# Prompt attention: four places for a head's queries and keys, sent for three heads ahead

## The chip, the cores and the metric

One core of a Trainium2 chip runs the whole program. The metric is the device time of one execution in microseconds; three runs of the kernel before are at hand, and one further execution was profiled.

## The reference, cut to what matters

The program is one step of a small decoder: a convolution mixer, shared keys, values and forget gates, and one attention layer, for a prompt of 1024 positions and for 8 single new positions that attend to a paged cache. The change lies in the prompt's attention, 16 heads of 64 features, in float32:

```python
def fox_attend(q, k, v, cq, ck, q_pos, k_pos):
    ...
    s = jnp.einsum('bqhd,bkhd->bhqk', qi.astype(jnp.float32), kf) * scale
    s = s + jnp.swapaxes(ci, 1, 2)[..., :, None] - ckh[..., None, :]
    s = jnp.where((k_pos[None, :] <= pi[:, None])[None, None], s, -jnp.inf)
    p = jax.nn.softmax(s, axis=-1)
    return jnp.einsum('bhqk,bkhd->bqhd', p, vf)

def fox_mixer(x, k, v, cq, ck, q_pos, k_pos, norm_g, w_in, q_g, w_out):
    ...
    o = fox_attend(q, k, v, cq, ck, q_pos, k_pos).reshape(b, t, ATTN_DIM)
    return x + (o * jax.nn.silu(z)) @ w_out
```

Here `c` is the running sum of the forget gates' logarithms, and `z` the output gate.

## The kernel before

Ahead of the attention, the projections leave queries, keys, values, gates and the sums `c` in HBM (`qt_scr`, `kt_scr`, `vt_scr`, `z_scr`, `c_scr`), the float32 ones as a high and a low part. The prompt's attention then runs from about 973 to 1333 us, and the output projection follows.

Each head goes through two passes. `first(h)` has 8 steps, one for a block of 128 queries: score matmuls into PSUM (L1165, L1166, and a mask, L1168), a row maximum on VectorE (L1169), an exponential with its sum on ScalarE (L1171). After four blocks, `logsum` turns maximum and sum into a row of normalisers, and SyncE sends it to two partitions of the head's `q2` (L1193, source `lt`). `second(h)` has 6 steps on transposed scores: matmuls into `st` (L1228, L1229, masks L1234, L1236), the exponential into `pt` on ScalarE (L1238), its high part `ph` on GpSimd (`pool_copy`, L198), its low part `pl` on GpSimd or VectorE (L1242), and three steps later (`LAGW`) the matmuls with the values into `po` (`weigh`, L1208, L1209). `po` goes to `og` (L1212, L1213); at the end of each odd head `og` is multiplied by the gates `sz` (L1255) and split for the output projection (L1257, L1258).

The two passes are laid side by side by a pattern of 14 turns (`PAT`): 8 first steps and 6 second steps, with the first passes 13 steps ahead (`LEAD`). So `first(h+2)` begins three first steps after `second(h)` has begun.

A head's `q1, q2, k1, k2` (16 KB of each partition) are one place. Pool `h0` has two and pool `hd` one; head h takes `hd` when `h % 3 == 2`. `load_qk(h)` sends 8 transfers from SyncE's queue (L639): six of 256 KB, then 16 KB and 24 KB from `c_scr`. `load_rest(h)` sends the values `vh` (512 KB, two buffers, L644) and, for even h, the gates `sz` of two heads (512 KB, two buffers, L648). Both are written down together for head h+2 where `second(h)` begins.

The program is laid out by a compiler that orders each engine's instructions by what it reckons to be ready; the order written in the source is its priority. An engine runs its own list strictly in order. A tile waits for the last reader of the tile that had its memory before. The pools lie on one another in the order in which they are opened: `ld` (`sz`), `hd`, `wk` (`og`, `pt`, `ph`, `pl`, `tb`), and the output projection's pool (`wr`, `wb`, values of the cache) later takes the same memory.

Of the kernel before, what the change touches and what calls it, by code (L numbers as in the profile page):

```python
# [9 lines left out]
F32 = mybir.dt.float32  # L10
F32R = mybir.dt.float32r
# [8 lines left out]
P = 128  # L20
D = 1024
T = 1024
# [3 lines left out]
NH = 16  # L26
# [50 lines left out]
QORD = (0, 4, 1, 5, 2, 6, 3, 7)  # L77
PS_S = 2
PS_O = 1
PTB = 4  # L80
PHB = 5
VHB = 2
LAGW = 3
PLO = ((0, 0), (0, 2), (1, 0), (1, 6))
# [41 lines left out]
def f32(ap):  # L126
    return ap.bitcast(F32)
# [7 lines left out]
def tile_step(ctx, tc, xt, st, stT, vecs, cwT, win, wout, wqkv, wf, wbo, hvec, qgf, ck, cv, cf, pt,  # L135
# [16 lines left out]
    def table(name):  # L152
        tc.keep_in_program_order(S.preload_act_table_set(name))
# [475 lines left out]
    hd = h0 = None  # L629
    szs = {}  # L630

    def load_qk(h):
        pool = hd if h % 3 == 2 else h0
        q1, q2, k1, k2 = [pool.tile([P, 1024], F32R, tag=nm, name=nm) for nm in ("q1", "q2", "k1", "k2")]
        fs = slice(h * HD, (h + 1) * HD)

        for out, src in ((q1[0:HD], qt_scr[0, fs]), (k1[0:HD], kt_scr[0, fs]), (q1[HD:P], qt_scr[1, fs]), (k1[HD:P], kt_scr[0, fs]),
                         (q2[0:HD], qt_scr[0, fs]), (k2[0:HD], kt_scr[1, fs]), (q2[HD:HD + 4], c_scr[h, 0:4]), (k2[HD:HD + 6], c_scr[h, 4:10])):
            SY.dma_start(out=f32(out), in_=src)  # L639
        return q1, q2, k1, k2  # L640

    def load_rest(h):
        vh = hd.tile([P, 8, P], F32R, tag="vh", name="vh", bufs=VHB)
        SY.dma_start(out=f32(vh), in_=vt_scr[h].rearrange("(i p) f -> p i f", p=P))  # L644
        hp, e = divmod(h, 2)
        if e == 0:
            sz = szs[hp] = ld.tile([P, T], F32, tag="sz", name="sz")
            SY.dma_start(out=sz, in_=z_scr[hp])  # L648
        return vh

    qk0 = []

    def load0():
        nonlocal h0
        h0 = pat.enter_context(tc.tile_pool(name="h0", bufs=2, side="right", reuse_waits="tile"))
        qk0.extend([load_qk(0), load_qk(1)])
# [48 lines left out]
    with ExitStack() as pb:  # L705
# [374 lines left out]
        for n_, (kind, half) in enumerate(order):  # L1080
            ws, nxt = nxt, None
            if n_ + 1 < len(order):
                k2, h2 = order[n_ + 1]
# [38 lines left out]
    with pat:  # L1122
        ld = pat.enter_context(tc.tile_pool(name="ld", bufs=2, reuse_waits="tile"))
        hd = pat.enter_context(tc.tile_pool(name="hd", bufs=1, reuse_waits="tile"))
# [6 lines left out]
        def qbank(name):  # L1131
            if OBANK:
                return psO.tile([P, 512], F32, tag="o", name=name)
            return psQ.tile([P, 512], F32, tag="q", name=name)

        ogs = {}

        def load(h):
            return load_qk(h) + (load_rest(h),)


        off_ = []

# [1 line left out]
        def put_off(n, f):  # L1145
            off_.append([n, f])

        def catch_up(n=1):
            for x in list(off_):
                x[0] -= n  # L1150
                if x[0] < 0:
                    off_.remove(x)
                    x[1]()

        def first(h, q1, q2, k1, k2, vh):
            nm = sm.tile([P, 8], F32, tag="nm", name="nm")
            sr = sm.tile([P, 8], F32, tag="sr", name="sr")
            for qi in QORD:
                nk = (qi + 1) * P
                qsl = slice(qi * P, (qi + 1) * P)  # L1160
                ss = qbank("ss") if nk in SMF else psS.tile([P, 1024], F32, tag="s", name="ss")
                for b0 in range(0, nk, 512):
                    w = min(512, nk - b0)
                    lastb = b0 + w == nk
                    PE.matmul(ss[:, b0:b0 + w], q1[:, qsl], k1[:, b0:b0 + w], start=True, stop=False)  # L1165
                    PE.matmul(ss[:, b0:b0 + w], q2[0:HD + 4, qsl], k2[0:HD + 4, b0:b0 + w], start=False, stop=not lastb)  # L1166
                    if lastb:
                        PE.matmul(ss[:, qsl], identb, maskb, start=False, stop=True)  # L1168
                V.tensor_reduce(out=nm[:, qi:qi + 1], in_=ss[:, :nk], axis=AX.X, op=ALU.max, negate=True)  # L1169
                def expsum(ss=ss, nk=nk, qi=qi):  # L1170
                    S.activation(out=ss[:, :nk], in_=ss[:, :nk], func=AF.Exp, bias=nm[:, qi:qi + 1], accum_out=sr[:, qi:qi + 1])  # L1171

                put_off(DEXP, expsum)
                catch_up()
                if qi % 4 == 3:
                    put_off(DEXP + DLS, lambda qi=qi: logsum(h, qi // 4, nm, sr, q2))
                yield nk

        def logsum(h, c, nm, sr, q2):
            cs = slice(c * 4, c * 4 + 4)  # L1180
            S.activation(out=sr[:, cs], in_=sr[:, cs], func=AF.Ln)
            V.tensor_tensor(out=nm[:, cs], in0=nm[:, cs], in1=sr[:, cs], op=ALU.subtract)
            lc = sm.tile([P, 8], F32R, tag="lc", name="lc")
            V.tensor_copy(out=lc[:, 0:4], in_=nm[:, cs])
            V.tensor_tensor(out=lc[:, 4:8], in0=nm[:, cs], in1=f32(lc[:, 0:4]), op=ALU.subtract)

            def turn():
                ps = qbank("lt")
                PE.transpose(f32r(ps[0:8, 0:P]), lc, identr)
                lt = sm.tile([8, P], F32, tag="lt", name="lt")  # L1190
                S.copy(out=lt, in_=ps[0:8, 0:P])
                for a in range(2):
                    SY.dma_start(out=f32(q2[HD + 4 + a:HD + 5 + a, c * 512:(c + 1) * 512]).rearrange("a (t q) -> a t q", t=4), in_=lt[4 * a:4 * a + 4])  # L1193

            put_off(DLT, turn)

        def second(h, q1, q2, k1, k2, vh):
# [17 lines left out]
            for c in range(2):  # L1215
                po = psO.tile([P, 512], F32, tag="o", name="po")
                for j0 in range(0, 4 * c + 4, 2):
# [12 lines left out]
                    for o in range(0, off, 512):  # L1230
# [4 lines left out]
                        elif ds:  # L1235
                            PE.matmul(st[:, ds[0]:ds[0] + P], identb, maskt, start=False, stop=True)  # L1236
                    pt_, ph, pl = [wk.tile([P, 1024], dt, tag=nm, name=nm, bufs=b) for nm, dt, b in (("pt", F32, PTB), ("ph", F32R, PHB), ("pl", F32R, PHB))]
                    S.activation(out=pt_[:, :off], in_=st[:, :off], func=AF.Exp)  # L1238
# [14 lines left out]
            if e:  # L1253
                for a, b in ((0, 512), (512, 1024)):
                    (V if a // 512 in OGV else G).tensor_tensor(out=og[:, a:b], in0=og[:, a:b], in1=szs[hp][:, a:b], op=ALU.mult)  # L1255
                for a, b in ((0, 512), (512, T)):
                    S.copy(out=oa.hi(hp, a, b - a), in_=og[:, a:b])  # L1257
                    V.tensor_tensor(out=oa.lo(hp, a, b - a), in0=og[:, a:b], in1=f32(oa.hi(hp, a, b - a)), op=ALU.subtract)  # L1258

        hs = [qk0[h] + (load_rest(h),) for h in range(2)]  # L1260
        table("natural_log_exp_and_others")
        oa = Act("o")

        def firsts():
            for h in range(NH):
                yield from first(h, *hs[h])

        def seconds():
            for h in range(NH):
                if h + 2 < NH:  # L1270
                    hs.append(load(h + 2))
                yield from second(h, *hs[h])


        if MAN:
            pat.enter_context(tc.manual_schedule(engines={getattr(mybir.EngineType, e) for e in MAN.split()}))
        fs_, ss_, n = firsts(), seconds(), 0
        for _ in range(LEAD):
            next(fs_)
# [138 lines left out]
```

## Time and profile before

| what | us |
|---|---|
| median of 3 runs (lowest, highest) | 1462.08 (1460.68, 1472.82) |
| the profiled execution's own time | 1459.9 |
| span of its trace | 1458.2 |

The span is what the trace covers, from the first to the last instruction; 1.7 us of the execution lie around it. In the views, PE is TensorE's matmuls, PEld its weight loads, DVE VectorE, ACT ScalarE, POOL GpSimd, and SPq SyncE's queue, from which all transfers of this stage are sent. PEclk is the granted clock of TensorE as a share of 2.4 GHz. A window's row gives its bounds and length, the busy time of PE, PEld, DVE, ACT and POOL with the number of instructions, the granted clock, the DMA engines' busy share and GB/s. A matmul's end is modelled and matmuls are pipelined, so a busy PE isn't a PE at its peak.

### The profile page before, as it was taken

What the parts mean: (1) busy time and instruction counts of PE and PEld (TensorE: products, weight loads), DVE (VectorE), ACT (ScalarE), POOL (GpSimd) and SP (SyncE); (2) the same over time, 40 slices, a digit from 0 to 9 for tenths busy, and PEclk for the clock granted to TensorE, in tenths of its full rate; (3) what the DMA queues carried; (4) which work ended last, traced back from release to release, by engine and by line L of the source; (5) the groups of instructions that cost most, each with busy time, mean ns of one, the idle gap of its engine ahead of it and who ended that gap; (6) DMA issues with size and microseconds to landing.
All of it is one profiled execution on the core that took longest, in us unless ns stands there. A gap on an engine that the chain in (4) does not pass through costs nothing.

```text
span 1458.2 us, 21461 instructions
## 1 busy us (share of the span) xinstructions
PE 1292.8 (89%) x6543; PEld 1077.8 (74%) x6543; DVE 1132.5 (78%) x1844; ACT 734.1 (50%) x1922; POOL 803.9 (55%) x603
## 2 busy tenths in 40 slices
PE   5999999789999999998898899897988888887978
PEld 5999999777777777666776778786766666665766
DVE  6999999998735699989898999854656575667841
ACT  7676537646645666655642232135656565662100
POOL 4699987862210253456565565724545455567930
PEclk9999999999999999999998989997868798888979
DMA  5111001121334576878778888693444456423841
GB/s 206 56 59 59 30 29 34 30 75 41 130 125 145 158 225 203 229 250 272 231 251 273 277 272 268 211 241 91 111 96 101 92 133 133 101 48 118 286 139 37
DMA packets 155530, 213.95 MB, mean 147 GB/s; under 512 B 14057, under 2 KB 82281, under 8 KB 155399
## 3 DMA queue, kind: packets, MB, share of 16 engines
q1 hardware_dynamic: 137879, 202.09, 47.4%
q10 hardware_dynamic: 16896, 8.39, 2.0%
q0 software_dynamic: 640, 2.10, 0.5%
q8 instruction: 52, 0.85, 0.3%
q14 instruction: 63, 0.52, 0.1%
HBM read 165.22 MB, written 48.13 MB: 146 GB/s over the span
## 4 chain that ended last, share of the span: by engine, by line
PE 18%; DMA 10%; DVE 10%; issue 5%; SPq 4%; ACT 2%; POOL 1%; DVEq 0%; ACTq 0%; POOLq 0%
DMA k<-c_scr 4%; DVE vt L683 4%; DMA vt<-in_cv 3%; SPq L639 2%; PE st L1228 2%; PE st L1229 2%; PE ss L1166 2%; PE ss L1165 2%; DMA k<-kt_scr 2%; PE po L1208 1%; PE po L1209 1%; PE py L1312 1%; PE py L1314 1%; PE py L1313 1%; PE pz L1055 1%
## 5 line engine op out<-in xcount | busy, mean ns | idle before, releaser
L347 POOL TENSOR_TENSOR cvt<-cvt 128x512 f32<-128x512 f32 (+4 forms) x179 | 243.7, 1394 | 38.4 <-ACT cvt L343 35.5
L906 POOL TENSOR_TENSOR kh<-kh,qb 128x512 f32<-128x512 f32 x96 | 139.8, 1472 | 135.6 <-DMA kh<-in_ck 85.4
L352 DVE SCALAR_TENSOR_TENSOR acc<-u,cw,acc 128x512 f32<-128x512 f32 (+4 forms) x285 | 196.0, 742 | 0.1
L198 POOL TENSOR_SCALAR ph<-pt 128x896 fp32r<-128x896 f32 (+1 forms) x96 | 87.6, 921 | 175.9 <-ACT pt L1238 172.3
L1169 DVE TENSOR_REDUCE nm<-ss 128x1 f32<-128x768 f32 (+7 forms) x128 | 93.6, 751 | 110.4 <-PE ss L1168 97.5
L685 POOL TENSOR_TENSOR av<-av,vt 128x512 f32<-128x512 f32 x80 | 134.2, 1698 | 69.8 <-DVE vt L683 53.0
L1105 PE MATMUL pq<-wp,acth 128*128 128x512 f32 x384 | 160.1, 417 | 0.0
L1107 PE MATMUL pq<-wp,actl 128*128 128x512 f32 x384 | 156.4, 407 | 0.0
L1106 PE MATMUL pq<-wp,acth 128*128 128x512 f32 x384 | 156.2, 407 | 0.0
L683 DVE TENSOR_TENSOR vt<-vt,lg 128x512 f32<-128x512 f32 x112 | 133.8, 1228 | 7.8 <-DMA vt<-in_cv 7.6
L343 ACT ACTIVATE cvt<-u,cw 128x512 f32<-128x512 f32 (+4 forms) x195 | 126.1, 719 | 17.9 <-POOL cvt L347 9.4
L1171 ACT ACTIVATE ss<-ss,nm 128x768 f32<-128x768 f32 (+7 forms) x128 | 91.2, 713 | 44.5 <-DVE nm L1169 43.4
L1238 ACT ACTIVATE pt<-st 128x896 f32<-128x896 f32 (+1 forms) x96 | 75.4, 809 | 71.7 <-PE st L1229 46.6
L1242 POOL TENSOR_TENSOR pl<-pt,ph 128x384 fp32r<-128x384 f32 (+2 forms) x56 | 105.7, 1894 | 2.7
L1165 PE MATMUL ss<-k,q 128*128 128x512 f32 (+2 forms) x192 | 80.2, 425 | 23.7 <-DMA k<-kt_scr 14.6
L1166 PE MATMUL ss<-k,q 68*128 68x512 f32 (+2 forms) x192 | 74.3, 400 | 20.4 <-DMA k<-c_scr 17.7
L1107 PEld LDWEIGHTS pq<-wp,actl 128*128 128x128 f32 x384 | 75.2, 196 | 19.2 <-issue 0.8
L1105 PEld LDWEIGHTS pq<-wp,acth 128*128 128x128 f32 x384 | 75.8, 197 | 18.0 <-ACT hsq L826 0.8
L1106 PEld LDWEIGHTS pq<-wp,acth 128*128 128x128 f32 x384 | 75.7, 197 | 16.9 <-issue 0.2
L907 DVE TENSOR_REDUCE lg<-kh 128x8 f32<-128x512 f32 x128 | 82.7, 673 | 5.0 <-POOL kh L906 5.0
L1208 PE MATMUL po<-ph,vh 128*128 128x512 f32 x192 | 78.3, 411 | 5.8 <-DVE og L1213 4.0
L1228 PE MATMUL st<-q,k 128*128 128x512 f32 (+1 forms) x192 | 79.5, 422 | 3.0 <-ACT ss L1171 2.9
(337 smaller groups left out, 3788.7 us busy)
## 6 DMA issues: line engine op xcount, KB each, us to landing
kh<-in_ck SPq DMA_DIRECT2D x128, 256.0 KB
vt<-in_cv SPq DMA_DIRECT2D x128, 256.0 KB
wraw<-in_wqkv SPq DMA_DIRECT2D x56, 256.0 KB
wr<-in_win SPq DMA_DIRECT2D x24, 512.0 KB
q<-qt_scr SPq DMA_DIRECT2D x48, 256.0 KB
k<-kt_scr SPq DMA_DIRECT2D x48, 256.0 KB
vt_scr<-vx SPq DMA_DIRECT2D x32, 256.0 KB
vh<-vt_scr SPq DMA_DIRECT2D x16, 512.0 KB
```

The lines of the kernel that those rows point to most:

```text
L343: S.activation(out=t[:, :m], in_=u[:, lo + j:hi + j], func=AF.Copy, scale=cw[:, c, j:j + 1])
L347: G.tensor_tensor(out=pacc[:, :m], in0=pacc[:, :m], in1=t[:, :m], op=ALU.add)
L352: V.scalar_tensor_tensor(out=acc, in0=u[:, lo + jd:hi + jd], scalar=cw[:, c, jd:jd + 1], in1=acc, op0=ALU.mult, op1=ALU.add)
L683: V.tensor_tensor(out=heads(vt[x] if g else ax), in0=heads(vt[x]), in1=over_d(lg[:, p0:p0 + 8], P, 8), op=ALU.mult)
L685: (V if g % VDVE == 3 else G).tensor_tensor(out=ax, in0=ax, in1=vt[x], op=ALU.add)
L906: (V if g % 4 == 3 else G).tensor_tensor(out=kt, in0=kt, in1=qb, op=ALU.mult)
L1105: PE.matmul(ps, na.hi(k, t * P, P), ws[k][:, 0:512], start=(k == 0), stop=False)
L1106: PE.matmul(ps, na.hi(k, t * P, P), ws[k][:, 512:1024], start=False, stop=False)
L1107: PE.matmul(ps, na.lo(k, t * P, P), ws[k][:, 0:512], start=False, stop=(k == KT - 1))
L1165: PE.matmul(ss[:, b0:b0 + w], q1[:, qsl], k1[:, b0:b0 + w], start=True, stop=False)
L1228: PE.matmul(st[:, o:o + w], k1[:, js], q1[:, qs], start=(o % 512 == 0), stop=False)
L1242: (G if plo else V).tensor_tensor(out=pl[:, :off], in0=pt_[:, :off], in1=f32(ph[:, :off]), op=ALU.subtract)
```

## The change

The places become four: two in `h0`, two in `hd`. `load_qk` is written down for head h+3 where `second(h)` begins, after the first three heads have been sent for ahead of the loop. `load_rest` is split off, and is written down for head h+1 there, ahead of `load_qk`. To make room for 16 KB, `pt` has three buffers instead of four (4 KB less), `ph` and `pl` four instead of five (8 KB less), and `sz` one instead of two (4 KB less). No instruction is added or removed.

```diff
-PTB = 4
-PHB = 5
+PTB = 3
+PHB = 4
...
     def load_qk(h):
-        pool = hd if h % 3 == 2 else h0
-        q1, q2, k1, k2 = [pool.tile([P, 1024], F32R, tag=nm, name=nm) for nm in ("q1", "q2", "k1", "k2")]
+        pool = hd if h % 4 > 1 else h0
+        q1, q2, k1, k2 = [pool.tile([P, 1024], F32R, tag=nm, name=nm, bufs=2) for nm in ("q1", "q2", "k1", "k2")]
...
-            sz = szs[hp] = ld.tile([P, T], F32, tag="sz", name="sz")
+            sz = szs[hp] = ld.tile([P, T], F32, tag="sz", name="sz", bufs=1)
...
-        def load(h):
-            return load_qk(h) + (load_rest(h),)
...
-        def first(h, q1, q2, k1, k2, vh):
+        def first(h, q1, q2, k1, k2):
...
-        hs = [qk0[h] + (load_rest(h),) for h in range(2)]
+        hs = qk0 + [load_qk(2)]
+        vhs = [load_rest(0)]
...
         def seconds():
             for h in range(NH):
-                if h + 2 < NH:
-                    hs.append(load(h + 2))
-                yield from second(h, *hs[h])
+                if h + 1 < NH:
+                    vhs.append(load_rest(h + 1))
+                if h + 3 < NH:
+                    hs.append(load_qk(h + 3))
+                yield from second(h, *hs[h], vhs[h])
```

## Rows read from the trace of the kernel before

**Rows 1.** Windows by head, cut where each head's first pass begins; columns as named above.
```profile
1057.50:1082.90 25.40, 22.61 (x88) 17.54 (x89) 13.86 (x25) 12.10 (x30) 10.21 (x7) 0.66 0.46 93
...
1194.70:1214.80 20.10, 17.75 (x101) 13.63 (x99) 15.27 (x21) 15.05 (x34) 14.33 (x12) 1.00 0.43 101
...
1259.30:1279.00 19.70, 15.41 (x89) 12.21 (x89) 15.75 (x22) 13.80 (x30) 15.11 (x13) 1.00 0.70 149
sum 290.20, PE 245.97 PEld 193.50 DVE 178.69 ACT 171.77 POOL 157.26; mean PE 18.92 PEld 14.88 DVE 13.74 ACT 13.21 POOL 12.10
```
**Rows 2.** PE's waits, 988.8 to 1279: total us, times, longest.
```profile
PE ss L1166 <- DMA k<-c_scr: 17.7, 10, 3.1
PE ss L1165 <- DMA k<-kt_scr: 14.6, 9, 2.9
PE ss L1165 <- ACT pt L1238: 6.6, 6, 1.5
PE ss L1166 <- DMA k<-kt_scr: 2.5, 2, 1.3
```
**Rows 3.** Timeline of PE, 984 to 993: start, us, what, wait before it.
```profile
985.16 0.39 PE L1166 MATMUL ss<-k,q 68*128 68x512 f32 x1
...
988.81 0.30 PE L1165 MATMUL ss<-k,q 128*128 128x128 f32 x1 [2.79 <-DMA k<-kt_scr]
...
990.65 0.78 PE L1229 MATMUL st<-q,k 70*128 70x512 f32 x1
```
**Rows 4.** The chain that ended last, head 7's load: start, us, what.
```profile
1098.37 0.17 SPq L639
...
1102.31 6.81 DMA k<-c_scr
```
**Rows 5.** PE's waits, 1194.6 to 1214.9.
```profile
PE ss L1165 <- DMA k<-kt_scr: 1.0, 1, 1.0
```
**Rows 6.** PE's waits, 1259.2 to 1279.1.
```profile
PE ss L1165 <- DMA k<-kt_scr: 2.1, 1, 2.1
...
PE ss L1166 <- DMA k<-c_scr: 1.4, 1, 1.4
```
**Rows 7.** Timeline of SyncE's queue, 940 to 1130.
```profile
985.12 0.34 SPq L648 DMA_DIRECT2D sz<-z_scr  x1
...
1003.85 0.51 SPq L639 DMA_DIRECT2D q<-qt_scr  x1
...
1014.26 0.40 SPq L644 DMA_DIRECT2D vh<-vt_scr  x1
...
1028.62 0.51 SPq L639 DMA_DIRECT2D q<-qt_scr  x1
...
1042.79 0.35 SPq L648 DMA_DIRECT2D sz<-z_scr  x1
```
**Rows 8.** SyncE's queue: its waits, 988.8 to 1279.
```profile
SPq L648 <- DVE og L1255: 11.3, 4, 3.4
```
**Rows 9.** Timeline of VectorE, 1097 to 1106.
```profile
1099.87 3.07 DVE L1242 TENSOR_TENSOR pl<-pt,ph 128x1024 fp32r<-128x1024 f32 x2
```
**Rows 10.** Timeline of ScalarE, 1097 to 1106.
```profile
1102.70 1.30 ACT L1238 ACTIVATE pt<-st 128x896 f32<-128x896 f32 x2 [1.36 <-PE st L1236]
```
**Rows 11.** Timeline of ScalarE, last head.
```profile
1319.22 1.30 ACT L1238 ACTIVATE pt<-st 128x896 f32<-128x896 f32 x2 [0.35 <-PE st L1236]
```
**Rows 12.** Timeline of GpSimd, last head.
```profile
1320.46 2.34 POOL L1242 TENSOR_TENSOR pl<-pt,ph 128x1024 fp32r<-128x1024 f32 x1
```
**Rows 13.** Timeline of SyncE's queue, 1255 to 1458.
```profile
1313.14 0.39 SPq L1299 DMA_DIRECT2D wbr<-in_wbo  x1
```
**Rows 14.** The chain that ended last, 1300 to 1458.
```profile
1312.47 1.60 DMA q<-lt
...
1332.10 0.70 DVE og L1255
```
**Rows 15.** Timeline of PE, output projection.
```profile
1392.99 0.76 PE L1312 MATMUL py<-wb,oh 128*128 128x512 f32 x1 [9.87 <-DVE xr L1317]
```

## The prediction

> **What bounds the kernel now.** I read first the source for where the change lies, then the windows over the attention cut by head, then TensorE's waits in that stretch, then the chain, and last the timelines of the queues that the change touches.
>
> The span is 1458.2 us, the execution 1459.9. From the first score matmul of head 2 (988.8) to that of head 15 (1279.0) lie 13 heads in 290.2 us, 22.32 us a head. No engine fills it: the sum row has TensorE at 18.92 us a head, VectorE 13.74, ScalarE 13.21, GpSimd 12.10 [rows 1]. So something is waited for, and TensorE's waits name it: those for a load of `k` make 17.7 + 14.6 + 2.5 = 34.8 us, the next one, for a score bank, 6.6 [rows 2]. One of them, 2.79 us, lies just ahead of 988.8 [rows 3], so 32.0 are inside, 2.46 a head.
>
> The chain shows how such a wait arises. SyncE starts head 7's load at 1098.37, when the scores of head 4's second pass are done with the place; the last of its eight transfers goes out at 1102.31 and lands 6.81 us later [rows 4]. That is 10.75 us, and the program has three of eight first steps between start and use, 3/8 x 22.32 = 8.4 us. So the load is late once a head.
>
> What a head takes when its load is less late must come from the heads that suffered least. Two of the 13 windows have a granted clock of 1.00, that is 2.4 GHz; the others lie lower, down to 0.66 [rows 1]. The clock goes with the waits: a 512-wide matmul takes 0.39 us ahead of the wait that ends at 988.81, and 0.78 just behind it [rows 3]. The first of the two took 20.1 us with 1.0 of load wait in it [rows 1, 5], the second 19.7 with 2.1 + 1.4 [rows 1, 6]: net 19.1 and 16.2, mean 17.65.
>
> **Queries and keys three heads ahead.** With four places, head h+3's load takes the place of head h-1, let go at the same moment as now, and is needed a head later: at the 18.75 us a head found below, 1.375 x 18.75 = 25.8 us after its start, against the 10.75 it takes. The slack of 15 us covers its transfer and its issue, so the load waits should all go. The eight issues stand where they stood on SyncE, ahead of or behind the same `lt` rows; what is new is only whose load they are. What a head gains has two bounds. If the waits close and nothing else changes, a head takes 22.32 - 2.46 = 19.86. If every head runs as the two at full clock did, net of their waits, 17.65. The lower one is flattered: in its windows VectorE had 15.27 and 15.75 us of work [rows 1], more than the mean, which had piled up behind a wait; and the 6.6 us of waits for a bank come sooner when TensorE does. The upper one leaves out the clock. Neither is nearer, so I take the middle, 18.75: 13 x (22.32 - 18.75) = 46.4 us, with 32.0 and 13 x 4.67 = 60.7 as bounds. That another wait fills the gap, down to nothing gained, is a rival below.
>
> **The start.** Head 2's load is now written ahead of the first `vh` and `sz` and so goes out earlier: its wait of 2.79 us [rows 3] can go. But its place lies in memory that the last projection's weights had, and which of them is read last shifts with the layout; no row prices that. Bounds: 2.8 gained; 4.5 lost, a third of 10.75 + 2.79. I take 2.8, since the load waits for that projection now too.
>
> **Values and gates apart.** `vh` of head h+1 takes the buffer of head h-1, as now, and is needed no sooner: nothing. `sz` has one buffer: the next pair's gates go only when the odd head's `og` has been multiplied, and are needed two heads later, so the transfer hides behind some 37 us. What can cost is its place on SyncE, where `load_qk` and the `lt` rows queue behind it. If the queue ran in the written order, it would stand on `sz` for most of a head. The timeline says that it doesn't: `vh` of head 2 is written ahead of `sz` of the second pair and of head 3's load, and goes out behind both, at 1014.26 against 985.12 and 1003.85 [rows 7]. What isn't ready is passed over. SyncE has waited for `og` in this way 11.3 us in four waits, 3.4 at most [rows 8], ahead of loads that now have 15 us to spare. I cost it at nothing; if an `lt` row that is needed at once stands behind each, it is 7 x 3.4 = 24.
>
> **Fewer `pt`, `ph`, `pl`.** The exponential of step k would wait for the low part of step k-3, not k-4. I set all 96 exponentials beside the low parts three before. Ahead of the last head the closest pair is in head 5: the low part ends at 1102.94 [rows 9], the exponential is the second of the two that begin at 1102.70 and end at 1104.00, and starts near 1103.5 [rows 10], 0.6 us free. Only in the last head, where second steps run alone, would some wait: its last exponential starts near 1320.0 [rows 11], the low part three before ends at 1322.80 [rows 12], 2.8 us. For `ph` and `pl`, the value matmuls four steps before stand ahead of the step's own scores in TensorE's list. I take 1.5 us at the end, between 0 and 2.8. With a head 3.57 us shorter, three of its six steps lose 1.8 us of slack, so the closest pairs may wait 1.2; in eight such heads 10 us at worst, which rival 1 holds.
>
> The Trainium skill, Perfetto Trace Analysis, Identifying Performance Opportunities, says that a gap which repeats on the engine that should be full can mean too little memory for the next tile. The trace agrees for the fourth place; the same rule speaks against taking buffers from `pt`, `ph` and `pl`, and by it the sum would be rival 1's 1444, by the rows above 1414.
>
> **The end.** The output weights' first buffers lie on `sz`. Now the first goes out at 1313.14 [rows 13], on gates that are done; with one `sz` it waits for the last product, which ends at 1332.80 [rows 14]. A sixth of a load's 10.75 us is 1.8, so the projection starts about that much later. TensorE stands for 9.87 us later in it, for VectorE [rows 15], which hides it; without that cover it costs 1.8. I take 1.5.
>
> **Sum.** 46.4 + 2.8 - 1.5 - 1.5 = 46.2: 1459.9 - 46 = 1414 us. The median of the runs lies 2.2 above the profiled execution, less than the runs differ; I leave it at 1414.
>
> **The rivals.** (1) Another wait takes the gap's place. For it: four engines have 12 to 19 us of work a head, and wide score tiles of both passes share PSUM; `pt`, `ph` and `pl` lose slack. Against it: the next wait is 6.6 us in 13 heads [rows 2]. If half of the 32.0 come back under other names and the clock doesn't rise, 16 are gained: 1444. (2) It doesn't do what it says: the loads of every second head stand on SyncE behind a waiting `sz` and come as late as now. Half of 32.0 gained, and 10 lost on the buffers: 1454. (3) Slower: SyncE stands on `sz` with the next head's `lt` rows behind it, and its second pass can't begin. Head 1's place is let go at 1028.62 and the gates behind its product go out at 1042.79 [rows 7], 14 us later; seven odd heads, between half and all of that: 50 to 98 us lost and the rest gained at most by half, so 1494 to 1542. It decides once SyncE stands on `sz` for longer than the 3.4 us seen. The order of rows 7 speaks against it.
>
> A second way to the slower side: 24 KB behind a load land 6.81 us after their issue [rows 4], a 2 KB `lt` row by itself 1.60 [rows 14]. If each head's `lt` fell right behind a load and were needed at once, 14 x 5.2 = 73 us: 1533. Against it: loads and `lt` rows follow each other in the queue now, and no wait for `lt` is among TensorE's longer ones. The Trainium skill, DMA: Bandwidth & Descriptors, Queues, rings and completion order, has a rule to this: a completion is written only when that DMA engine's earlier writes have landed. The two durations agree with it.
>
> **How the numbers follow.** The forecast, with its bounds of 60.7 + 2.8 and 32.0 - 4.5 - 4.6, lies between 1396 and 1437 and has 0.58; still better, 0.04; rival 1 above that, 0.20; no change within 1%, rival 2 among it, 0.10; rival 3 and the `lt` rows, 0.08. The range from 1396 to 1447 holds 0.78. About 1%, 14.6 us, is what a measurement of this kernel can tell from no change. Faster by more: 0.58 + 0.04 + 0.20 = 0.82; the same 0.10; slower 0.08.
>
> **What would show it.** Right: no load of `k` among TensorE's waits from head 3 on; 18 to 19.9 us a head; most windows at a clock of 0.9 or above; loads that start 20 us or more ahead of use; `sz` on SyncE behind `load_qk`. Wrong: waits of ScalarE for `pl` of over 1 us a head, bank waits of TensorE above 1.5 us a head, SyncE on `sz` for more than 5 us, or an attention that starts over 3 us later. The compiler lays out all engines' lists anew, so an order that differs elsewhere in the stage could move the time by some microseconds either way with none of these.

## The result, and the profile after

The changed kernel takes 1448.8 us (median of 16 runs, 1431.4 to 1460.1), the kernel before 1462.8 in 16 runs beside them: a ratio of 0.988, 95% interval 0.9855 to 0.9909. The ratios, here and in the table below, leave out runs over 1.5% above the fastest of their kernel, so they aren't the quotients of the medians. The change makes the kernel faster, by not quite a third of what was forecast. The profiled execution takes 1444.2 us, its span 1442.5, 15.7 less than before. In the changed source the lines of the attention stand three lower: L1182 is the line that was L1185.

Cut by the first score matmul of heads 0, 3 and 15, by the last product of `og` and by the end, the stretches of the span compare so:

| stretch | before | after | difference |
|---|---|---|---|
| up to head 0 | 973.5 | 980.5 | +7.0 |
| head 0 to head 3 | 38.0 | 40.0 | +2.0 |
| head 3 to head 15 | 267.5 | 241.6 | -25.9 |
| head 15 to the last product | 53.8 | 55.7 | +1.9 |
| from there to the end | 125.4 | 124.7 | -0.7 |

The first row isn't the change: the four compute engines have the same lists up to the attention, SyncE's differs only in the last microsecond ahead of it, and two kernels below that have every list of after came to head 0 at 974.5 and 983.5. The rest is taken as the change's; how far two profiles of the same lists differ in it is said with the table. The middle one as windows, before and after, and two windows of single heads of after, to be held beside [rows 1] (the columns are the same):

```profile
1011.50:1279.00 267.50, 227.35 (x1070) 178.85 (x1070) 167.50 (x248) 160.80 (x353) 145.59 (x117) 0.82 0.50 110
```

```profile
1020.50:1262.10 241.60, 206.13 (x1060) 156.96 (x1061) 190.02 (x251) 158.32 (x353) 145.30 (x117) 0.93 0.53 118
...
1061.30:1078.30 17.00, 15.25 (x89) 11.83 (x88) 13.52 (x20) 11.54 (x27) 10.09 (x9) 1.00 0.47 108
...
1196.60:1221.10 24.50, 20.21 (x89) 14.97 (x89) 18.61 (x24) 15.88 (x35) 13.72 (x11) 0.82 0.66 142
```

Twelve heads take 20.13 us each in place of 22.29. The granted clock is 0.93, not 0.82. VectorE is busy 22.5 us longer with the same work. TensorE's waits in the same stretch of after (total, times, longest):

```profile
PE lt L1186 <- DVE lc L1182: 21.8, 17, 2.4
PE ss L1162 <- ACT ss L1168: 9.2, 11, 0.9
```

The loads of `k`, which led [rows 2], are gone. At the head of the list stands a wait that was 2.4 us in all before (`PE lt L1189 <- DVE lc L1185: 2.4, 2, 1.5`): `lt`, the transpose that turns a head's normalisers for `q2`, waits for `lc`, a subtraction of 128x4 numbers on VectorE. All 24 records of that subtraction in the stretch, as min/median/max in ns, before and after:

```profile
L1185 DVE TENSOR_TENSOR lc<-nm,lc x24: 161/162/1099, 1024.1 to 1277.4; 128x4 fp32r<-128x4 f32 x24
```

```profile
L1182 DVE TENSOR_TENSOR lc<-nm,lc x24: 142/1178/2223, 1024.5 to 1252.4; 128x4 fp32r<-128x4 f32 x24
```

The timelines of VectorE, GpSimd and TensorE around one of the longest waits, each in its own fence:

```profile
1090.43 1.00 DVE L1179 TENSOR_TENSOR nm<-nm,sr 128x4 f32<-128x4 f32 x1
1091.46 0.17 DVE L1181 CAST lc<-nm 128x4 fp32r<-128x4 f32 x1
1091.66 2.20 DVE L1182 TENSOR_TENSOR lc<-nm,lc 128x4 fp32r<-128x4 f32 x1
```

```profile
1089.93 1.49 POOL L198 TENSOR_SCALAR ph<-pt 128x1024 fp32r<-128x1024 f32 x1
1091.50 2.34 POOL L1239 TENSOR_TENSOR pl<-pt,ph 128x1024 fp32r<-128x1024 f32 x1
```

```profile
1093.91 0.22 PE L1186 MATMUL lt<-identr,lc 128*8 128x128 f32 x1 [2.36 <-DVE lc L1182]
```

Read them together. The subtraction `nm` begins while GpSimd writes `ph` and ends with it, at 1091.4. The cast runs in the gap between GpSimd's two operations in its usual 0.17 us. `lc` begins 0.16 us after `pl` and ends with it, at 1093.84. So a subtraction that takes 0.16 us by itself takes as long as what is left of GpSimd's operation, and TensorE, whose list has the transpose next, stands for 2.36 us. In heads 3 to 15 of after, 12 of the 24 `lc` take 2.19 to 2.22 us; each begins 0.16 or 0.17 us after such a `pl` and ends with it, and the other 12 begin while GpSimd is idle. In all, the 24 take 28.3 us in place of 6.1, which is nearly all of VectorE's 22.5.

At the start another wait has come. TensorE's waits from head 0 to head 3, the copies of head 0's `lt` on ScalarE (first and last start), and SyncE's queue:

```profile
PE st L1226 <- DMA q<-lt: 9.4, 1, 9.4
```

```profile
L1188 ACT COPY lt<-lt x2: 238/246/255, 990.7 to 992.2; 8x128 f32<-8x128 f32 x2
```

```profile
987.71 3.37 SPq L639 DMA_DIRECT2D q<-qt_scr  x1
...
998.27 0.28 SPq L639 DMA_DIRECT2D k<-c_scr  x1
999.16 17.59 SPq L1190 DMA_DIRECT2D q<-lt  x8
```

Head 0's rows were ready at 992.5, and went out at 999.16, behind the eight transfers of head 3's load; its second pass began at 1005.1.

The theory to test, **P**: the fourth place removed the waits for loads; GpSimd's `pl` and `ph` then held small VectorE operations in front of TensorE, through a path to SBUF (the memory that the engines work in) that both engines use. Its rivals: **V**, VectorE simply has too much to do (79% busy), and `lc` is only the last in its list; **B**, the buffers taken from `pt`, `ph` and `pl` cost the time.

### The profile page after: what moved, and what is told of

The parts are those of the page before. It is cut to its first block, busy times and chain, and to the rows that moved or that the text cites. A ratio compares the mean times of both kernels' runs of the same rounds, so it can differ in the third digit from the quotient of the medians.

```text
span 1442.5 us, 21436 instructions
## 1 busy us (share of the span) xinstructions
PE 1266.6 (88%) x6543; PEld 1050.8 (73%) x6543; DVE 1151.2 (80%) x1844; ACT 732.2 (51%) x1922; POOL 800.8 (56%) x603
## 5 line engine op out<-in xcount | busy, mean ns | idle before, releaser
L198 POOL TENSOR_SCALAR ph<-pt 128x896 fp32r<-128x896 f32 (+1 forms) x96 | 90.7, 960 | 153.3 <-ACT pt L1235 139.7
L1166 DVE TENSOR_REDUCE nm<-ss 128x1 f32<-128x128 f32 (+7 forms) x128 | 93.3, 750 | 75.5 <-PE ss L1165 62.7
L683 DVE TENSOR_TENSOR vt<-vt,lg 128x512 f32<-128x512 f32 x112 | 127.8, 1173 | 13.4 <-DMA vt<-in_cv 13.2
L1168 ACT ACTIVATE ss<-ss,nm 128x128 f32<-128x128 f32 (+7 forms) x128 | 91.1, 712 | 68.6 <-DVE nm L1166 68.3
L1162 PE MATMUL ss<-k,q 128*128 128x512 f32 (+2 forms) x192 | 78.9, 411 | 13.6 <-ACT ss L1168 12.6
L1235 ACT ACTIVATE pt<-st 128x896 f32<-128x896 f32 (+1 forms) x96 | 75.5, 805 | 30.1 <-PE st L1233 19.4
L1107 PEld LDWEIGHTS pq<-wp,actl 128*128 128x128 f32 x384 | 74.3, 193 | 18.7 <-issue 0.8
L1205 PE MATMUL po<-ph,vh 128*128 128x512 f32 x192 | 72.4, 382 | 7.8 <-DVE og L1210 4.5
L1226 PE MATMUL st<-q,k 70*128 70x512 f32 (+1 forms) x192 | 67.1, 367 | 9.8 <-DMA q<-lt 9.8
L1225 PE MATMUL st<-q,k 128*128 128x512 f32 (+1 forms) x192 | 72.4, 384 | 2.3 <-ACT pt L1235 2.1
```

Source lines behind the costliest of these rows:

```text
L198: G.tensor_scalar(out=out, in0=in_, scalar1=1.0, scalar2=1.0, op0=ALU.mult, op1=ALU.mult)
L683: V.tensor_tensor(out=heads(vt[x] if g else ax), in0=heads(vt[x]), in1=over_d(lg[:, p0:p0 + 8], P, 8), op=ALU.mult)
L1107: PE.matmul(ps, na.lo(k, t * P, P), ws[k][:, 0:512], start=False, stop=(k == KT - 1))
```

## The experiments

Heads are those from 3 to 15, in us each. The next three columns are for that stretch: its granted clock, and TensorE's waits for loads of `k` and for `lc` (`nm` where the edit has no `lc`). The last is the stretch from head 0 to head 3. These columns come from one profile of each kernel; onein and sf have the lists of after in every engine, and their heads take 20.68 and 20.02 us beside 20.13, and their starts 38.8 and 40.8 beside 40.0; so differences below about 0.7 us a head, or 2 us in the start, say nothing.

| kernel | median us | ratio to before, 95% | head | clock | loads | `lc` | start |
|---|---|---|---|---|---|---|---|
| before | 1462.8 | | 22.29 | 0.82 | 30.9 | 2.4 | 38.0 |
| after | 1448.8 | 0.9855 to 0.9909 | 20.13 | 0.93 | none | 21.8 | 40.0 |
| onein | 1448.8 | 0.988 to 0.995 | 20.68 | 0.91 | none | 22.1 | 38.8 |
| redlc | 1416.3 | 0.959 to 0.974 | 17.49 | 0.98 | none | 4.6 | 39.3 |
| tr32 | 1411.2 | 0.960 to 0.972 | 17.42 | 1.00 | none | 3.5 | 38.3 |
| btr32 | 1451.5 | 0.989 to 0.996 | 21.23 | 0.85 | 30.1 | none | 40.4 |
| bbuf | 1450.9 | 0.989 to 0.995 | 21.18 | 0.87 | 24.4 | 8.4 | 39.5 |
| three | 1451.9 | 0.989 to 0.996 | 20.83 | 0.88 | 22.3 | 7.2 | 40.1 |
| pt4 | 1428.1 | 0.970 to 0.982 | 19.23 | 0.91 | none | 11.5 | 39.3 |
| sf | 1444.4 | 0.980 to 0.995 | 20.02 | 0.91 | none | 18.0 | 40.8 |
| gate | 1430.9 | 0.970 to 0.983 | 19.08 | 0.94 | none | 15.2 | 35.0 |
| trgate | 1408.4 | 0.956 to 0.966 | 17.34 | 1.00 | none | 4.2 | 35.5 |
| mansp | 1539.5 | 1.042 to 1.057 | 27.38 | 0.76 | 54.2 | 9.0 | 31.7 |
| tr32sp | 1528.3 | 1.034 to 1.050 | 27.05 | 0.75 | 53.0 | 5.3 | 30.7 |

**onein: one input in place of two.**

```diff
-            V.tensor_tensor(out=lc[:, 4:8], in0=nm[:, cs], in1=f32(lc[:, 0:4]), op=ALU.subtract)
+            V.tensor_scalar(out=lc[:, 4:8], in0=f32(lc[:, 0:4]), scalar1=0.0, scalar2=1.0, op0=ALU.mult, op1=ALU.mult)
```

> The changed kernel with one instruction replaced: VectorE's subtraction lc = nm - lc (two inputs in SBUF) becomes an operation of the same size with one input, which writes zeros; so the rounding remainder of the log-sum is left out of the output. The order of every engine's list is that of the changed kernel. Theory P (GpSimd's ph and pl hold the two-input subtraction through the memory port that they share): lc falls from up to 2.2 us to under 0.25 us wherever pl runs, the waits of PE's lt for lc from 24.0 us to under 5, heads 3 to 15 from 20.1 us each to 18.6 (18.0 to 19.2), the time from 1449 to about 1430. Rival V (VectorE has too much to do, and lc is only the last in its list): lc falls but what waits behind it takes the time, 20.1 us a head stays within 0.5, the time stays within 6 us of 1449. Rival B (the cut from four and five buffers to three and four): nothing changes, 20.1 us.

Nothing changed by more than profiles of the same lists differ. The records of the replaced operation in heads 3 to 15:

```profile
L1182 DVE TENSOR_SCALAR lc<-lc x24: 149/1184/2236, 1017.3 to 1251.8; 128x4 fp32r<-128x4 f32 x24
```

So P as I had put it, a hold of operations with two inputs, falls: the product with one input is held as long, 2.24 us. V and B stood. The trace of after had a row that decides what to try next: VectorE's reductions keep their length beside GpSimd; the one over 128x640 takes 0.81 to 0.83 us in all 16 records, 14 of them begun while `ph` or `pl` ran. Those read score banks in PSUM; the next run puts a reduction of numbers in SBUF in the place of `lc`.

**redlc: the same place, a reduction.**

```diff
-            V.tensor_tensor(out=lc[:, 4:8], in0=nm[:, cs], in1=f32(lc[:, 0:4]), op=ALU.subtract)
+            V.tensor_reduce(out=lc[:, 4:8], in_=f32(lc[:, 0:4]).unsqueeze(2), axis=AX.X, op=ALU.max)
```

> The changed kernel with the subtraction of lc replaced by a reduction of the same 128x4 size over one input in SBUF; the order of every engine's list stays that of the changed kernel. In the place of the rounding remainder it writes the high part a second time, so the log-sum goes into the output twice. In the run before, an operation with one input (a product with constants) was held as long as the subtraction (2.2 us), while reductions of VectorE kept their length beside GpSimd in every record (0.82 us for 128x640 with and without). Theory P2 (GpSimd's ph and pl hold copies, casts, products with constants and two-input operations of VectorE, and not reductions): the reduction takes under 0.4 us everywhere, PE's waits for lc fall from 24.0 us to under 5, the clock of heads 3 to 15 rises from 0.93 to over 0.97, a head takes 17.4 to 18.6 us, the time is 1412 to 1432. Rival Q (VectorE's operations on SBUF are all held, whatever their kind): 2.2 us again, 20.1 to 20.7 us a head, time within 6 us of 1449.

Record by record, all engines have the lists of after, and only the kind of this one small operation differs. Its records, TensorE's wait for it and the window of heads 3 to 15:

```profile
L1182 DVE TENSOR_REDUCE lc<-lc x24: 135/157/158, 1026.8 to 1227.5; 128x4 fp32r<-128x4 f32 x24
```

```profile
PE lt L1186 <- DVE lc L1182: 4.6, 10, 0.8
```

```profile
1022.80:1232.70 209.90, 192.54 (x1063) 148.99 (x1062) 168.27 (x249) 156.61 (x350) 152.67 (x116) 0.98 0.62 136
```

The reduction never takes more than 0.16 us, though 16 of the 24 begin while GpSimd runs. The heads lose 31.7 us: TensorE's wait for `lc` is 17.2 shorter, its busy time 13.6, at a clock of 0.98 in place of 0.93. V and B fall as the cause of these 31.7 us: VectorE's list and all buffers are those of after. P holds in the form that the expectation gave it, P2, all of whose figures came. The Trainium skill, SBUF — State Buffer, Who interferes with whom, says that VectorE and GpSimd share one pair of SBUF ports, that whoever issues first has it for a whole instruction, and that copies, casts, products with constants and operations with two SBUF inputs can want it while reductions on this chip never do. By that rule, the trace agrees in each point that these runs touch: 2.20 us for the subtraction, 2.24 for the product, 0.16 for the reduction, and the end of each hold at the end of GpSimd's operation. The ports themselves no trace shows.

**tr32: the whole computation without that operation.** The normalisers are transposed first, and split into high and low part from PSUM.

```diff
-            lc = sm.tile([P, 8], F32R, tag="lc", name="lc")
-            V.tensor_copy(out=lc[:, 0:4], in_=nm[:, cs])
-            V.tensor_tensor(out=lc[:, 4:8], in0=nm[:, cs], in1=f32(lc[:, 0:4]), op=ALU.subtract)
...
-                PE.transpose(f32r(ps[0:8, 0:P]), lc, identr)
-                lt = sm.tile([8, P], F32, tag="lt", name="lt")
-                S.copy(out=lt, in_=ps[0:8, 0:P])
+                PE.transpose(ps[0:4, 0:P], nm[:, cs], ident)
+                lh = sm.tile([4, P], F32R, tag="lh", name="lh")
+                S.copy(out=lh, in_=ps[0:4, 0:P])
+                ll = sm.tile([4, P], F32R, tag="ll", name="ll")
+                V.tensor_tensor(out=ll, in0=ps[0:4, 0:P], in1=f32(lh), op=ALU.subtract)
...
```

> The changed kernel, whole computation: the fp32 log-sum is transposed, and the split into high and low part is made behind the transpose, from PSUM, 4x128 in place of 128x4: the subtraction has one input in PSUM and one in SBUF. Theory P: no wait of PE for lc, what may be left is a hold of nm (its subtraction still has two inputs in SBUF) of under 1 us a head; heads 3 to 15 at 18.3 to 19.3 us, time 1425 to 1438. Rival V or B: heads stay at 19.8 to 20.5 us, time within 6 us of 1449. The planner writes a new order for every engine here, which may add or take some us of itself.

It beat the expectation: 1411.2 us, and every head from 4 on at about 17 to 18 us. The window of heads 3 to 15, and the longest wait of TensorE in it that VectorE ends:

```profile
1013.70:1222.70 209.00, 188.62 (x1062) 146.58 (x1061) 167.75 (x225) 157.55 (x353) 152.63 (x116) 1.00 0.61 137
```

```profile
PE lt L1182 <- DVE nm L1179: 3.5, 5, 0.7
```

The subtraction behind the transpose, with one input in PSUM, and the one ahead of it, with two in SBUF, in the same stretch:

```profile
L1186 DVE TENSOR_TENSOR ll<-lt,lh x24: 268/278/279, 1023.1 to 1217.7; 4x128 fp32r<-4x128 f32 x24
L1179 DVE TENSOR_TENSOR nm<-nm,sr x24: 144/232/1935, 1017.3 to 1215.6; 128x4 f32<-128x4 f32 x24
```

Of the 24 `ll`, 18 begin while GpSimd runs, and none is longer for it. `nm` is still held, for up to 1.94 us; but TensorE waits for it 3.5 us in all. So the edit doesn't end the holds, it takes the one away that TensorE stood on.

**btr32: the same edit in the kernel before.**

> The kernel before (three places, everything of a head sent two heads ahead) with the log-sum split behind the transpose, the whole computation. With the same edit the changed kernel takes 1411 us, 17.4 us a head. Theory P2 (the change removes the waits for loads, and the hold of lc ate two thirds of that): without the hold the kernel before still waits for its loads, 20 to 30 us in heads 3 to 15, at a clock of 0.82 to 0.88; 21 to 22.3 us a head, time 1448 to 1463; the change would then be worth 37 to 52 us. Rival L (the edit of the split is what speeds both kernels up, and four places bring no more than they did): time about 1425, ratio as large as in the changed kernel (0.966 to 0.975).

The kernel before gains 0.4 to 1.2%, no more, and waits for its loads as it did; heads 3 to 15:

```profile
PE ss L1166 <- DMA k<-c_scr: 21.0, 12, 2.5
PE ss L1165 <- DMA k<-kt_scr: 9.1, 11, 1.3
```

So rival L falls. With `lc` out of the way the change is worth 1451.5 - 1411.2 = 40.3 us (0.966 / 0.992 = 0.974, or 38 us, by the ratios, whose kernel before ran beside each), with it 14. Both kernels have lists of their own, which, as three runs below show, can move a time by 12 us or more; so the 40 is no exact figure. Each kernel has its own wall; the one behind the loads was `lc`.

**bbuf and three: parts of the change.** bbuf is the kernel before with `PTB = 3` and `PHB = 4`; three is the changed kernel with the three places back.

```diff
-        pool = hd if h % 4 > 1 else h0
+        pool = hd if h % 3 == 2 else h0
...
-                if h + 3 < NH:
-                    hs.append(load_qk(h + 3))
+                if h + 2 < NH:
+                    hs.append(load_qk(h + 2))
```

> The kernel before with the buffers of the change and nothing else of it: pt in three places (four before), ph and pl in four (five before). Theory P: the buffers are no part of what the change lost; heads 3 to 15 at 22.3 us, 21.8 to 22.8, time within 5 us of 1463. Rival B: exp or ph waits for a place, heads at 23 us or more, time 1470 or more.

> The changed kernel with three places for queries and keys, sent two heads ahead as before; values and gates still sent apart, one head ahead, and the smaller buffers. It tells which part of the change took the waits for loads away. If the fourth place did: PE waits 20 us or more for the c_scr and kt_scr loads in heads 3 to 15, clock under 0.88, 21 to 22.3 us a head, time 1448 to 1463. If sending the values and gates apart did (the loads of queries and keys then have the queues to themselves): waits for loads under 10 us, time under 1445.

three keeps its waits for loads, 22.3 us in heads 3 to 15, so the fourth place, with the load that it lets go out a head earlier, is what removed them; the clock, 0.88, and the heads, 20.83, lie just outside what was expected for this case:

```profile
PE ss L1163 <- DMA k<-c_scr: 15.2, 10, 2.5
PE lt L1186 <- DVE lc L1182: 7.2, 6, 2.2
PE ss L1162 <- DMA k<-kt_scr: 5.2, 9, 1.4
```

But in time it is only 3 us slower than after, and the two intervals overlap: the place took away 22 us of load waits and brought 14.6 of `lc`. bbuf went against both theories: the smaller buffers alone made the kernel 0.5 to 1.1% faster, at a clock of 0.87 in place of 0.82 and with 6.5 us less of load waits. Nothing in the edit explains why the loads came less late; what comes with it is another order of every engine's list.

**pt4: `pt` in four places again.** `PTB = 4` in the changed kernel.

> The changed kernel with pt in four places, as the kernel before had, in place of three (ph and pl stay in four; five don't fit). The buffers alone, cut in the kernel before, made it 0.8% faster, 21.2 us a head in place of 22.3, against both theories, and with another order of every engine's list by the planner. Theory P2: pt's place is no bound; what changes is only which VectorE operation the order puts beside GpSimd's pl; 19.5 to 21 us a head, PE's waits for lc 15 to 30 us, time 1440 to 1455. Rival B (three places of pt cost the changed kernel time): under 19 us a head, under 1435.

It is 21 us faster than after, as B said, though its heads, 19.23, miss B's range as well as P2's. B's reason isn't in the trace: in heads 3 to 15 of after ScalarE doesn't wait for `pl` at all, so no place of `pt` was missing as the kernel ran. TensorE's waits in pt4 show what differs, half of the wait for `lc`:

```profile
PE lt L1186 <- DVE lc L1182: 11.5, 8, 2.7
PE ss L1162 <- ACT pt L1235: 5.0, 4, 1.5
```

The new lists set fewer `lc` beside GpSimd's work: 6 of 24 are held, not 12. All three of P2's ranges were missed at their lower ends. What the lists themselves owe to the count of places, no run shows.

**sf and gate: head 0's rows ahead of head 3's load.** sf writes the load down later:

```diff
-                yield from second(h, *hs[h], vhs[h])
+                for i, x in enumerate(second(h, *hs[h], vhs[h])):
+                    if h == 0 and i == 2:
+                        hs.append(load_qk(3))
+                    yield x
```

> The changed kernel with one move: head 3's eight query and key loads are sent after the third step of the first head's second pass, no longer ahead of it, so that head 0's lt rows do not stand behind them on SyncE. If that queueing is what costs the start: PE's wait for lt (9.4 us) falls under 2, the stretch from head 0's to head 3's first matmul falls from 40.0 us to 31 to 33, with the clock higher in it, and the time to about 1440. Rival: the start is bound by the loads themselves (heads 1, 2 and 3 have to come in anyway); then PE waits the same 8 to 10 us for another load, and the stretch stays at 38 to 41.

The compiler put the load where it had been, with nothing to hold it back: every engine's list is that of after, and the wait is 9.8 us. So sf tested nothing of the start; its 1444.4 us are a second sample of after. gate holds the load by data:

```diff
+        for y in (q1, q2, k1, k2) if gate is not None else ():
+            for p in (0, HD):
+                V.tensor_copy(out=y[p:p + 1, 0:1], in_=gate)
...
+                if h == 0 and c == 1:
+                    hs.append(load_qk(3, lt[0:1, 0:1]))
```

> The changed kernel with head 3's query and key loads held back until head 0's second lt is copied: eight copies of one element each write from lt into the load's places on VectorE, so that the planner has to put head 0's four lt rows ahead of these eight transfers on SyncE; whole computation. If the queueing behind head 3's load is what costs the start: the rows are issued before 993 on the changed kernel's clock in place of 999.2, PE's wait for lt falls from 9.4 us to under 4, head 0 to head 3 takes 31 to 35 us in place of 40 (31.7 with SyncE in program order), heads 3 to 15 stay at 20.1, time 1439 to 1445. Rival: the rows' transfers stand behind head 2's load in the queues, PE waits 8 us or more still; or head 3's first matmul waits for its load instead; time within 3 us of 1449.

Head 0 begins at 985.6 in this profile, so the rows go out 10.5 us after it and not 18.7; TensorE's wait, below SyncE's queue:

```profile
996.05 2.66 SPq L1193 DMA_DIRECT2D q<-lt  x4
998.81 0.51 SPq L642 DMA_DIRECT2D q<-qt_scr  x1
```

```profile
PE st L1231 <- DMA q<-lt: 4.6, 1, 4.6
```

The start falls from 40.0 to 35.0: the queueing cost about 5 of the 9.4 us, and 4.6 of the wait stay, not under 4 as expected. The further 13 us, which weren't expected, are in the heads, 19.08 each with 15.2 us of `lc`: another order again.

**trgate: both edits together.**

> The changed kernel with both edits: the log-sum split behind its transpose, and head 3's load held back until head 0's second transpose is copied; whole computation. If both costs are independent: heads 3 to 15 at 17.4 us at a clock of 0.99 or more, head 0 to head 3 at 31 to 34 us in place of 38.3, time 1403 to 1407. If the start is bound by something else: 1409 to 1413, as with the first edit alone.

1408.4 us, the lowest of all, between the two cases of the expectation. The heads are as fast as in tr32 and the start is 2.8 us shorter, 35.5 and not the 31 to 34 expected; the times can't tell the two kernels apart (their intervals overlap), so that the two gains add up isn't shown.

**mansp and tr32sp: SyncE in the written order.** `MAN = "SP"` in after and in tr32.

> The changed kernel with SyncE's list in the attention written in program order and not in the planner's: head 0's lt rows then stand ahead of head 3's loads. (Sending head 3's loads later in the program alone left SyncE's list as it was: the rows again came behind them, 9.8 us.) If that queueing costs the start: PE's wait for lt falls from 9.4 us to under 3, head 0 to head 3 takes 31 to 34 us in place of 40; heads 3 to 15 stay near 20.1 us; time 1440 to 1444. Rival: program order puts other loads late and SyncE stands on a buffer with lt rows behind it, over 1455.

> The changed kernel with both edits: the log-sum split behind its transpose, and SyncE's list in program order. If the two costs are independent: 17.4 us a head, the start 31 to 34 us in place of 38, time about 1404 to 1407. If program order brings waits of SyncE: over 1415.

The start came down to 31.7 and 30.7 us as expected; the rest is the rival. SyncE's longest wait in heads 3 to 15 of mansp, a piece of its queue, and TensorE's waits:

```profile
SPq L648 <- DVE og L1252: 128.8, 6, 22.3
```

```profile
1045.77 0.34 SPq L648 DMA_DIRECT2D sz<-z_scr  x1
1046.16 0.51 SPq L639 DMA_DIRECT2D q<-qt_scr  x1
...
1051.24 4.21 SPq L1190 DMA_DIRECT2D q<-lt  x4
```

```profile
PE ss L1162 <- DMA k<-kt_scr: 45.7, 6, 7.8
```

SyncE stands on the gates for up to 22.3 us until the product of `og` is done, and the next head's load and `lt` rows go out behind them. With the change, the compiler's order of SyncE's queue is worth 91 us.

## Why the prediction was wrong

**The likeliest case failed at one step: "Neither is nearer, so I take the middle, 18.75."** What stands ahead of that step held. The load waits all went, the clock came back to 0.88 or more in all but one of the twelve heads, and the lower bound of 17.65, read from two heads at full clock and called flattered, is what the stage can do: 17.42 in tr32, 17.49 in redlc. But heads took 20.13, above even the bound of 19.86, at which only the waits close. That bound took for granted that nothing new is waited for, and against rival 1 I put only that "the next wait is 6.6 us in 13 heads", as the kernel before had it. It is rival 1 that came, "another wait takes the gap's place"; the wait wasn't among those that I had named for it (banks of PSUM, places of `pt`), and of my signs of being wrong none that belongs to the change showed. That rival 1's 1444 lies near 1448.8 is in part luck: it has half of the load waits come back at an unchanged clock, and of 30.9 us 21.8 came back as `lc`, more than half, at a clock that rose to 0.93. I had set VectorE's work against the head's length as busy time and never asked how long its small operations are when GpSimd runs. The trace of before had the sign. Its small operations were held too, here the cast that writes `lc`, which takes 0.17 us by itself:

```profile
L1184 DVE CAST lc<-nm x30: 155/170/1483, 992.1 to 1307.6; 128x4 fp32r<-128x4 f32 x30
```

Of the 24 `lc` themselves 3 were held there, 1.1 us at most, and TensorE waited 2.4 us for them in twelve heads; in after it was 12, for 2.2 us. Whether the new order of the lists or the faster TensorE set them beside `pl`, no run separates.

**The start** was to gain 2.8 us and lost 2.0. Head 2's load wait did go, and up to head 2 the 2.8 us came (12.5 us from head 0, not 15.3); from there to head 3 it lost 4.8, by the wait for the `lt` rows. (Profiles of the same lists lost 0.8 to 2.8 in all.) That head 3's load, now sent ahead of the loop, would stand before head 0's `lt` rows on SyncE, I had weighed only as a slower way for each head (an `lt` row behind a load), and held to be unlikely; it happened once, at the start, and gate got 5.0 us back by undoing it.

**Values and gates** at nothing was right. SyncE waited for `og` 1.4 us in all, in place of 11.3 [rows 8], and rival 2 didn't come. The point from which rival 3 decides was right too: made to stand on `sz`, the kernel takes 1539.5 us, inside the 1494 to 1542. Its price came out by other terms, though: SyncE stood six times for 21.5 us on average, not seven times for 7 to 14.

**Fewer `pt`, `ph`, `pl`** cost by their waits what was said where it was said: ScalarE's exponentials wait for `pl` 6.1 us in the whole stage, none of it in heads 3 to 15, and the stretch behind head 15 is 1.9 longer (1.5 forecast). What a count of places does to the lists, 12 us in bbuf and 21 in pt4, in opposite directions, the prediction had left at "some microseconds either way".

**The end** was to lose 1.5 and lost nothing: the first output weights go out at 1317.81, when the last product is done, and the projection's first matmul comes 2.2 us later behind that product than before; TensorE's later wait for VectorE, which was 9.87 [rows 15] and is 7.21, hides it.

In sum: of the 46.4 us forecast between head 2 and head 15, 21.1 came (269.1 us, not 290.2), 25.9 gained from head 3 on and 4.8 lost ahead of it. What the change could give was there, some 40 us, behind a second wall.

What stays open is why the kernel with only smaller buffers, and pt4 and gate beyond their own edits, are 12 to 21 us faster than their neighbours. Each has new lists on every engine and other waits for loads or `lc` with them; no run held the lists and changed the buffers.

## What to carry to other kernels

Where a wait is removed, list not only the engines' busy times but the small operations that stand between two engines on the way to the bottleneck, and look in the trace for one that was ever many times its usual length: it may be the next wall. In this kernel a tiny VectorE cast, product or two-input subtraction in SBUF took as long as what was left of the GpSimd operation beside it; a reduction, or an input in PSUM, got round it. A move in the source moved nothing in the planned lists (sf) until data held it there (gate), and an order that no one wrote can be what makes a change safe (mansp).

## What the runs showed of the hardware

A 128x4 product with constants, one input, was held for 2.24 us by GpSimd, as long as a subtraction with two; a reduction of the same numbers took 0.16 us beside the same work, and a 4x128 subtraction with one input in PSUM at most 0.28 (tr32). Waits of 21.8 us, spread as 17 pieces of at most 2.4 over 241.6 us, came with a granted clock of 0.93; with 4.6 us in their place it was 0.98, and 1.00 in tr32. So these short waits cost nearly twice their length in these profiles: between after and redlc, 31.7 us of heads for 17.2 us of waits.
